# Attention in chunks of 64 tokens, with 64 x 64 products on quarters of TensorE's array

## The chip, the cores and the metric

The kernel runs on one core of a Trainium2 chip. The metric is device time in microseconds for one call. All inputs are float32; the big projections are computed in three passes on rounded halves, the attention products in plain f32.

## What is computed

Two layers over 2048 tokens of width 1024. Each projects the tokens, runs two groups of heads side by side, gates them, projects back and normalises. The change touches only the attention-like group of each layer: gated linear attention (GLA) in layer 0, retention in layer 1, both with 4 heads, key width 64 and value width 128. Cut to that part:

```python
def _gla(q, k, v, log_a):                       # layer 0, chunks of 64 tokens
    b = jnp.cumsum(log_a.reshape(B, n, C, H, dk), axis=2)
    q_dec, k_dec = q * jnp.exp(b), k * jnp.exp(-b)
    scores = jnp.where(causal, jnp.einsum('bnihd,bnjhd->bnhij', q_dec, k_dec), 0.0)
    o_intra = jnp.einsum('bnhij,bnjhe->bnihe', scores, v)
    k_state = k * jnp.exp(b_last[:, :, None] - b)
    chunk_state = jnp.einsum('bnjhd,bnjhe->bnhde', k_state, v)
    s_in = _chunk_scan(jnp.exp(b_last)[..., None], chunk_state)   # S <- decay * S + chunk_state
    return o_intra + jnp.einsum('bnihd,bnhde->bnihe', q_dec, s_in)

def _retention(q, k, v):                        # layer 1, the same form, a fixed decay per head
    scores = jnp.einsum('bnihd,bnjhd->bnhij', q, k) * dmat        # dmat: decay, causal
    o_intra = jnp.einsum('bnhij,bnjhe->bnihe', scores, v)
    chunk_state = jnp.einsum('bnjhd,hj,bnjhe->bnhde', k, w_state, v)
    return o_intra + jnp.einsum('bnihd,hi,bnhde->bnihe', q, w_inter, s_in)
```

The chunk length is free: a longer chunk does more inside the masked product, a shorter one more through the state.

## The kernel before

The tokens come in 4 blocks of 512 (`NB`), each of 4 tiles of 128 (`NT`). Per block the kernel runs layer 0 and then layer 1. A projection is a `unit`: 8 slices of the contraction (`kt`) times three passes, for two output tiles at a time, into PSUM tiles `big` (4 of them). Most of its matmuls are 512 wide; the first two units of layer 0 are 272 and 256 wide. Weights stream in as `raw` and are split by `cut` (ScalarE rounds, L89; VectorE subtracts, L90).

The order on every engine is that of the program text (the schedule is manual). Small work is put between projection matmuls: `later(fn, delay)` queues a step, and `between()`, called after each 24 wide matmuls of a two-tile unit, runs the steps that are due, in the order in which they were queued.

`attend` is used by both layers. It queues one `first` step and 4 `outputs` steps, one per tile. Heads are counted h = 2s + r: s says which 128-wide half of the keys holds the head, r whether its 64 key rows lie in partitions 0 to 63 or 64 to 127. `first` computes tile 0's scores (L357, `att<-G` or `att<-qkT`) and masks them into `pm`. `outputs(t)` does on TensorE:
- masked scores times values (`att<-v,pm`): 4 products with 128 rows and 128 columns;
- queries times state (`att<-s,G`, `att<-s,qkT`): 4 products with 64 rows;
- the next tile's scores (`att<-G`): 4 products with 64 rows, not in the last step;
- this tile's chunk states (L393, `trp<-v,G` or `trp<-v,ks`): 4 products with 64 columns.

Then come `norm` (statistics; in layer 0 squares on ScalarE, in layer 1 on VectorE, then GpSimd), the state update (an add, and the decay in `upd`), the mask for the next tile (L372), and `scale`, which reads the output out of PSUM. Scores and outputs of one step share two PSUM tiles `att`, one per r; each step takes both again. PSUM tiles `trp` (2 of them) serve the chunk states, transposes and small products.

The operands: in layer 0 `values` are copied from PSUM by ScalarE (L458, L487) and state keys are transposed by TensorE (L507) and copied (L508); in layer 1 values are copied at L700, and rotated keys by VectorE at L659.

Of the kernel before, what the change touches and what calls it, by code (L numbers as in the profile page):

```python
# [17 lines left out]
P = 128  # L18
# [33 lines left out]
def trunk(ctx, tc, x, xT, pos, wv, w, w_a2, pvec, rowp, sgu_rows, w_sT, w_pool, ropec, poolc, out):  # L52
    nc = tc.nc
# [12 lines left out]
    const = ctx.enter_context(tc.tile_pool(name="const", bufs=1))  # L66
# [77 lines left out]
    def later(fn, delay=1):  # L144
        steps.append([delay, fn])
# [63 lines left out]
    def layer_norm_out(xs, rows, lnrow, after, cuts=1):  # L209
# [6 lines left out]
        def evac(half, t, ps):  # L216
# [4 lines left out]
            if half == 1:  # L221
# [31 lines left out]
    pm = [const.tile([P, 4, P], F32, name=f"pm{i}") for i in range(2)]  # L253
# [18 lines left out]
    g128 = rope[:, 40:42]  # L272
# [11 lines left out]
    for kt in range(KT):  # L284
# [4 lines left out]
        t = wpool.tile([P, 2, 512], F32R, tag="w", name="wt")  # L289
# [61 lines left out]
            delay += 1  # L351


    def attend(qk, vt, state, upd, norm, delay):

        def mm(dst, lhsT, rhs, start=False, stop=False):
            nc.tensor.matmul(dst, lhsT=lhsT, rhs=rhs, start=start, stop=stop, skip_group_check=True)  # L357

        def banks():


            return [ps_s.tile([P, 4, P], F32, tag="s", name="att") for _ in range(2)]

        def scores(t, ps, start):
# [5 lines left out]
        def masked(t, ps):  # L370
            for r in range(2):
                nc.vector.copy_predicated(pm[t % 2][:, r::2, :], mask_b, ps[r][:, 2:4, :])  # L372

        def first():
            ps = banks()
            scores(0, ps, True)
            masked(0, ps)

        def outputs(t):
            v, m, ps = vt(t), pm[t % 2], banks()  # L380
            last = t == NT - 1
            for h in range(4):
                mm(ps[h % 2][:, h // 2, :], m[:, h, :], v[:, h * P:(h + 1) * P], start=h < 2)
            for s in range(2):
                for r in range(2):
                    b0 = 64 * r
                    mm(ps[r][:, s, :], qk(s, b0, t)[1], state[b0:b0 + 64, s, :], stop=last and s == 1)
            if not last:
                scores(t + 1, ps, False)
            u = tr()  # L390
            for h in range(4):
                s, b0 = h // 2, 64 * (h % 2)
                nc.tensor.matmul(u[b0:b0 + 64, s, :], lhsT=qk(s, b0, t)[2], rhs=v[:, h * P:(h + 1) * P],  # L393
                                 start=True, stop=True)
            scale = norm(t, [p_[:, 0:2, :] for p_ in ps])
            nc.vector.tensor_tensor(state, state, u[:, 0:2, :], op=ALU.add)
            upd(t)
            if not last:
                masked(t + 1, ps)
            scale()  # L400

        later(first, delay)
        for t in range(NT):
            later(lambda t=t: outputs(t), delay + 2 * t + 1)


    def gla_decay(alrT):
# [37 lines left out]
    def layer0(b, xs):  # L445

        vt = r8.tile([P, NT, 512], F32, tag="r8", name="v0")
        alrT = w2("alrT")[0:48, :].bitcast(F32R)
        als, logs, decays, heads = [], [], [], {}
        f = small.tile([P, 2, NT], F32, tag="f", name="f", bufs=2)  # L450

        def evac_v0(t, ps):
# [3 lines left out]
            nc.vector.tensor_copy(al[:, 32:48], al[:, 0:16])  # L456
            als.append(al)
            nc.scalar.activation(vt[:, t, 0:256], ps[:, 0:256], AF.Copy)  # L458

        def low_rank():  # L460
            pa = tr()
# [22 lines left out]
        later(low_rank, 1)  # L484
        later(decay, 2)
        later(decay2, 3)
        unit(xs, lambda t, ps: nc.scalar.activation(vt[:, t, 256:512], ps, AF.Copy), True, cols=256)  # L487


        held = {}  # L490
# [1 line left out]
        def evac_qk(n, ps):  # L492
            held[n] = ps
            if n % 2 == 0:
                return
            s = n // 2
            psq, psk = held[n - 1], ps

            G = r8.tile([P, 3, TB], F32, tag="r8", name=f"G{s}")
            e, ei, _ = decays[s]  # L500
            nc.vector.tensor_tensor(G[:, 1, :], psk, ei, op=ALU.mult)
            nc.vector.tensor_tensor(G[:, 0, :], psq, e, op=ALU.mult)

            def state_keys():
                pt = tr()
                for t in range(NT):
                    nc.tensor.transpose(pt[:, t, :], G[:, 1, t * P:(t + 1) * P], ident)  # L507
# [6 lines left out]

        def qk(s, b0, t):
            G, rows_, cols_ = heads[s], slice(b0, b0 + 64), slice(t * P, (t + 1) * P)
            return G[rows_, 1, cols_], G[rows_, 0, cols_], G[:, 2, t * P + b0:t * P + b0 + 64]

        def upd(t):
            nc.vector.tensor_tensor(s0, s0, f[:, :, t:t + 1].broadcast_to([P, 2, P]), op=ALU.mult)  # L520


        o1 = vt
# [86 lines left out]
        for i in range(2):  # L610
            r = r8.tile([P, 2, D], F32, tag="r8", name="rows")
# [23 lines left out]
    def layer1(b, xs, rows):  # L635

        qkT = z8.tile([P, NT, 4, P], F32, tag="z8", name="qkT")
        ks = [w2(f"ks{i}").rearrange("p (t c) -> p t c", c=256) for i in range(2)]
        kst = [ks[t // 2][:, t % 2, :] for t in range(NT)]
# [4 lines left out]
        def rotate(t, ps):  # L644
            g = b * NT + t
            a = w2("ra")
            s_ = w2("rs_")

            nc.scalar.activation(a[:, 0:256], ps[:, 0:256], AF.Copy)
            nc.vector.tensor_tensor(a[:, 256:512].rearrange("p (h c) -> p h c", c=64),  # L650
                                    ps[:, 256:512].rearrange("p (h c) -> p h c", c=64),
                                    gam[:, 4:8].unsqueeze(2).broadcast_to([P, 4, 64]), op=ALU.mult)
            a3 = a.rearrange("p (h c) -> p h c", c=32)
            s3 = s_.rearrange("p (h c) -> p h c", c=32)
            nc.vector.tensor_tensor(s3, a3, sin[:, g:g + 1, :].broadcast_to([P, 16, 32]), op=ALU.mult)
            nc.vector.tensor_tensor(a3, a3, cos[:, g:g + 1, :].broadcast_to([P, 16, 32]), op=ALU.mult)
            nc.vector.tensor_tensor(a3[:, 0::2, :], a3[:, 0::2, :], s3[:, 1::2, :], op=ALU.subtract)
            nc.vector.tensor_tensor(a3[:, 1::2, :], a3[:, 1::2, :], s3[:, 0::2, :], op=ALU.add)
            nc.vector.tensor_copy(kst[t], a[:, 256:512])  # L659

            def turn():
                pt = tr()
                for s in range(4):
                    nc.tensor.transpose(pt[:, s, :], a[:, s * P:(s + 1) * P], ident)  # L664
# [5 lines left out]

        def qk(s, b0, t):
            b1 = b0 + 64
            return qkT[b0:b1, t, 2 + s, :], qkT[b0:b1, t, s, :], kst[t][:, s * P + b0:s * P + b1]

        def upd(t):
            nc.vector.tensor_tensor(s1, s1, g128.unsqueeze(2).broadcast_to([P, 2, P]), op=ALU.mult)

# [176 lines left out]
```

## Time and profile before

| | |
|---|---|
| time, median of 3 runs | 1503.72 us (1502.76 to 1504.43) |
| the profiled execution | 1503.44 us, its span 1501.7 us |
| TensorE matmul, busy | 1482.5 us, 99% |
| VectorE, busy | 930.1 us, 62% |
| ScalarE, busy | 551.5 us, 37% |
| GpSimd, busy | 125.1 us, 8% |
| granted TensorE clock, mean | 0.996 |

In the rows of the profile, PE is TensorE's matmul, PEld its weight load, DVE is VectorE, ACT ScalarE, POOL GpSimd. A row of the timeline has the start and the length in us, the engine, the line, the operation, out<-in with the shape, and how many instructions were merged. "64*128" on a matmul is rows by columns of the stationary operand. An f32 product shows as two matmul records, a projection pass as one. A row of the groups has busy time, mean ns of one, and after the second bar the idle time of the engine just before them, with what ended it.

### The profile page before, as it was taken

How to read it: one execution, taken by the hardware profiler on the slowest of the kernel's cores; microseconds unless marked ns; L12 is line 12 of the kernel's file. 1: busy time of each engine (PE TensorE's matmuls, PEld its weight loads, DVE VectorE, ACT ScalarE, POOL GpSimd, SP SyncE). 2: the span in 40 equal slices, each digit the busy share in tenths (PEclk: the TensorE clock that was granted, in tenths of full speed). 3: DMA queues.
4: the chain of work that ended last, by engine and by line, in shares of the span. 5: the costliest groups of instructions: out<-in, count | busy, mean ns of one | idle time of the engine just before them, and what ended most of it. 6: DMA issues, size and time to landing. Idle time of an engine off the chain costs nothing.

```text
span 1501.7 us, 20886 instructions
## 1 busy us (share of the span) xinstructions
PE 1482.5 (99%) x7728; PEld 1246.0 (83%) x7728; DVE 930.1 (62%) x1856; ACT 551.5 (37%) x956; POOL 125.1 (8%) x184
## 2 busy tenths in 40 slices
PE   7999999999999999999999999999999999999997
PEld 6888888888988888888898888888889888888886
DVE  4586486656655458576665546857576554684755
ACT  5434323333543332334263342323426334142430
POOL 1020010000101001010111100000010110100002
PEclk9999999999999999999999999999999999999999
DMA  7324322225523341313453343132435315232321
GB/s 236 99 85 136 117 85 85 85 57 163 177 83 105 120 141 57 113 57 107 131 171 99 84 133 120 59 111 65 142 107 168 111 57 167 86 93 76 97 79 56
DMA packets 87046, 162.18 MB, mean 108 GB/s; under 512 B 10096, under 2 KB 18336, under 8 KB 86944
## 3 DMA queue, kind: packets, MB, share of 16 engines
q1 hardware_dynamic: 86944, 160.85, 34.6%
q8 instruction: 60, 0.98, 0.3%
q14 instruction: 42, 0.34, 0.1%
HBM read 152.43 MB, written 8.39 MB: 107 GB/s over the span
## 4 chain that ended last, share of the span: by engine, by line
PE 96%; DMA 2%; DVE 1%; issue 0%; POOL 0%; ACT 0%; SPq 0%; DVEq 0%; POOLq 0%; ACTq 0%
PE big L181 86%; PE att L357 4%; PE trp L393 1%; PE trp L574 1%; PE trp L626 1%; PE trp L716 1%; DMA xraw<-in_xT 1%; DMA raw<-in_w 1%; PE trp L664 0%; PE trp L752 0%; PE trp L601 0%; DVE wt L90 0%; DMA raw<-in_wv 0%; PE trp L507 0%; SPq L109 0%
## 5 line engine op out<-in xcount | busy, mean ns | idle before, releaser
L181 PE MATMUL big<-wt,T 128*128 128x512 f32 (+2 forms) x3456 | 726.2, 370 | 10.7 <-ACT v L458 5.9
L181 PEld LDWEIGHTS big<-wt,T 128*128 128x128 f32 x3456 | 599.5, 190 | 117.5 <-ACT v L458 6.2
L181 PE MATMUL big<-T,wt 128*128 128x512 f32 x2688 | 625.9, 392 | 0.0
L181 PEld LDWEIGHTS big<-T,wt 128*128 128x128 f32 x2688 | 500.9, 188 | 106.0 <-issue 2.7
L90 DVE TENSOR_TENSOR wt<-raw,wt 128x512 fp32r<-128x512 f32 (+1 forms) x496 | 320.7, 673 | 233.1 <-ACT wt L89 231.9
L89 ACT ACTIVATE wt<-raw 128x512 fp32r<-128x512 f32 (+1 forms) x496 | 297.8, 616 | 359.1 <-PE big L181 251.5
L198 POOL TENSOR_SCALAR lnrs<-lnmv 128x1 f32<-128x1 f32 x32 | 33.4, 1042 | 618.3 <-DVE lnmv L223 618.3
L219 DVE SCALAR_TENSOR_TENSOR rows<-rows,big 128x512 f32<-128x512 f32 x64 | 43.7, 682 | 55.6 <-PE big L181 55.6
L201 POOL TENSOR_TENSOR rs<-rs,neghalf 128x4 f32<-128x4 f32 x48 | 58.4, 1216 | 3.9
L628 ACT ACTIVATE T<-trp 128x512 fp32r<-128x512 f32 x32 | 17.4, 595 | 106.3 <-PE trp L626 106.3
L231 DVE SCALAR_TENSOR_TENSOR rows<-rows,lnrs,ln 128x1024 f32<-128x1024 f32 (+1 forms) x36 | 41.6, 1165 | 19.5 <-POOL lnrs L201 18.6
L220 DVE BATCH_NORM_STATS2 lnst<-rows 128x6 f32<-128x512 f32 x64 | 44.5, 695 | 2.2
L228 DVE SCALAR_TENSOR_TENSOR rows<-rows,lnmv,ln 128x1024 f32<-128x1024 f32 x32 | 41.0, 1283 | 0.9
L206 DVE SCALAR_TENSOR_TENSOR y<-trp,pv,sg 128x512 f32<-128x512 f32 x48 | 33.8, 745 | 12.4 <-PE trp L601 7.0
L372 DVE COPY_PREDICATED pm<-mask,att 128x256 f32<-128x256 int32 x64 | 24.6, 440 | 27.1 <-PE att L357 27.1
L724 ACT ACTIVATE pb<-big 128x512 f32<-128x512 f32 x16 | 9.4, 590 | 76.4 <-PE big L181 76.4
L586 ACT ACTIVATE act<-big 128x512 f32<-128x512 f32 x32 | 18.3, 597 | 51.7 <-PE big L181 50.9
L687 DVE BATCH_NORM_STATS2 st<-att 128x6 f32<-128x128 f32 x64 | 14.2, 286 | 35.4 <-PE att L357 35.4
L357 PEld LDWEIGHTS att<-v,pm 128*128 128x128 f32 x256 | 33.5, 191 | 2.4
L552 DVE BATCH_NORM_STATS2 st<-zt 128x6 f32<-128x128 f32 x64 | 13.7, 277 | 35.0 <-ACT zt L548 35.0
L729 DVE TENSOR_TENSOR pl<-pb 128x527 f32<-128x527 f32 x16 | 11.3, 708 | 38.6 <-ACT pb L724 37.8
L89 ACT ACTIVATE T<-y 128x512 fp32r<-128x512 f32 x48 | 29.4, 627 | 15.7 <-DVE y L206 15.3
(184 smaller groups left out, 903.7 us busy)
## 6 DMA issues: line engine op xcount, KB each, us to landing
raw<-in_w SPq DMA_DIRECT2D x448, 256.0 KB, 2.8
xraw<-in_xT SPq DMA_DIRECT2D x32, 256.0 KB, 3.5
rows<-in_x SPq DMA_DIRECT2D x8, 1024.0 KB, 7.5
ln<-in_rowp SPq DMA_DIRECT2D x16, 512.0 KB, 6.3
out<-rows SPq DMA_DIRECT2D x12, 512.0 KB, 2.7
raw<-in_wv SPq DMA_DIRECT2D x32, 136.0 KB, 3.3
raw<-in_wv SPq DMA_DIRECT2D x32, 128.0 KB, 3.0
out<-rows SPq DMA_DIRECT2D x8, 256.0 KB, 2.0
```

The costliest lines, as they stand in the source:

```text
L89: nc.scalar.activation(hi, src, AF.Copy)
L90: nc.vector.tensor_tensor(lo, src, hi.bitcast(F32), op=ALU.subtract)
L181: nc.tensor.matmul(p_, lhsT=lhsT, rhs=rhs, start=(kt == 0 and q == 0), stop=(kt == KT - 1 and q == 2))
L198: nc.gpsimd.tensor_scalar(dst, var, eps, None, op0=ALU.add)
L201: nc.gpsimd.tensor_tensor(dst, dst, neghalf[:, :n], op=ALU.pow)
L206: nc.vector.scalar_tensor_tensor(y, psT, gain, sil, op0=ALU.mult, op1=ALU.mult)
L219: nc.vector.scalar_tensor_tensor(rh, rh, ALPHA, ps, op0=ALU.mult, op1=ALU.add)
L220: nc.vector.bn_stats(sts[t][:, half, :], rh)
L228: nc.vector.scalar_tensor_tensor(row, row, mv[:, 0:1], gt, op0=ALU.subtract, op1=ALU.mult)
L231: nc.vector.scalar_tensor_tensor(row[:, cs], row[:, cs], rs, bt[:, cs], op0=ALU.mult, op1=ALU.add)
L357: nc.tensor.matmul(dst, lhsT=lhsT, rhs=rhs, start=start, stop=stop, skip_group_check=True)
L372: nc.vector.copy_predicated(pm[t % 2][:, r::2, :], mask_b, ps[r][:, 2:4, :])
```

## The change

A tile of 128 tokens becomes two chunks of 64, c = 0 and 1. Every attention product becomes two or more of 64 rows by 64 columns, addressed by (r, c): r picks the array's rows, c its columns. For the values and state keys this needs odd heads (r = 1) in partitions 64 to 127 and even heads in 0 to 63, for both chunks; so copies that were one instruction become four (`by_heads`). The exception is the scores, where r picks both the rows and the output partitions.

The state now has a middle value: `s_mid` after the first chunk, and two alternating ends, `state` and `s_odd`. Chunk states of tile t + 1 are computed in `outputs(t)`, those of tile 0 in `first`, and added in `prepare`, so the state stands a tile ahead. The last step has no chunk states. Chunk states take both `trp` tiles instead of one.

```diff
-    mask_b = mask.bitcast(I32).unsqueeze(1).broadcast_to([P, 2, P])
+    nc.gpsimd.tensor_copy(mask[64:128, 0:64], mask[64:128, 64:128])
+    mask_b = mask.bitcast(I32)[:, 0:64].unsqueeze(1).broadcast_to([P, 4, 64])
...
+    def by_heads(copy, dst, src):
+        for r in range(2):
+            for c in range(2):
+                copy(r, dst(r, c), src(c, r))
...
         def scores(t, ps, start):
-            for s in range(2):
-                for r in range(2):
-                    k, q = qk(s, 64 * r, t)[:2]
-                    mm(ps[r][:, 2 + s, :], k, q, start=start and s == 0, stop=s == 1)
+            for c in range(2):
+                for s in range(2):
+                    for r in range(2):
+                        k, q = qk(s, 64 * r, t)
+                        mm(ps[r][half(r), 2 + c, half(s)], k[:, half(c)], q[:, half(c)],
+                           start=start and c == 0 and s == 0, stop=True)
+        def chunk_states(t):
+            u = [tr(), tr()]
+            for s in range(2):
+                for c in range(2):
+                    for r in range(2):
+                        mm(u[r][half(c), s, :], kt(s, r, c, t), vals(t, s, r, c), start=s == 0, stop=True)
+            return u
+        def prepare(t, ps, u):
+            after = states[(t + 1) % 2]
+            for r in range(2):
+                nc.vector.copy_predicated(pm[t % 2][half(r)], mask_b[half(r)],
+                                          ps[r][half(r), 2:4, :].rearrange("p c (s i) -> p (c s) i", i=64))
+            for dst, src, c in ((s_mid, states[t % 2], 0), (after, s_mid, 1)):
+                for r in range(2):
+                    nc.vector.tensor_tensor(dst[half(r)], src[half(r)], u[r][half(c), 0:2, :], op=ALU.add)
+            upd(t, after)
...
         def outputs(t):
-            for h in range(4):
-                mm(ps[h % 2][:, h // 2, :], m[:, h, :], v[:, h * P:(h + 1) * P], start=h < 2)
             for s in range(2):
-                for r in range(2):
-                    mm(ps[r][:, s, :], qk(s, b0, t)[1], state[b0:b0 + 64, s, :], stop=last and s == 1)
+                for c in range(2):
+                    for r in range(2):
+                        mm(ps[r][half(c), s, :], m[half(r), 2 * c + s, :], vals(t, s, r, c), start=s == 0)
+            for s in range(2):
+                for c in range(2):
+                    for r in range(2):
+                        mm(ps[r][half(c), s, :], qk(s, 64 * r, t)[1][:, half(c)],
+                           (states[t % 2], s_mid)[c][half(r), s, :], stop=True)
             if not last:
                 scores(t + 1, ps, False)
-            u = tr()
-            for h in range(4):
-                nc.tensor.matmul(u[b0:b0 + 64, s, :], lhsT=qk(s, b0, t)[2], rhs=v[:, h * P:(h + 1) * P],
-                                 start=True, stop=True)
+                u = chunk_states(t + 1)
             scale = norm(t, [p_[:, 0:2, :] for p_ in ps])
-            nc.vector.tensor_tensor(state, state, u[:, 0:2, :], op=ALU.add)
-            upd(t)
             if not last:
-                masked(t + 1, ps)
+                prepare(t + 1, ps, u)
             scale()
...
-            nc.scalar.activation(vt[:, t, 0:256], ps[:, 0:256], AF.Copy)
+            values(t, ps, 0)
...
-                nc.scalar.activation(G[:, 2, :], flat(pt), AF.Copy)
+                kt4 = G[:, 2, :].rearrange("p (t c i) -> p t c i", c=2, i=64)
+                by_heads(act_copy, lambda r, c: kt4[half(r), :, c, :], lambda c, r: pt[half(c), :, half(r)])
...
-        attend(qk, lambda t: vt[:, t, :], s0, upd, norm, 2)
+        attend(qk, kt, lambda t: vt[:, t, :], s0, upd, norm, (2, 3, 5, 7, 9))
...
-            nc.vector.tensor_copy(kst[t], a[:, 256:512])
+            by_heads(dve_copy, lambda r, c: kd[half(r), c], lambda c, r: ka[half(c), :, r, :])
...
-        attend(qk, lambda t: vts[t], s1, upd, norm, 2)
-        unit(xs, lambda t, ps: nc.scalar.activation(vts[t], ps, AF.Copy), True)
+        attend(qk, kt, lambda t: vts[t], s1, upd, norm, (3, 4, 5, 7, 9))
+        unit(xs, values, True)
```

All matmuls of `attend` now have one line, L385. In layer 0's first block the values' first half is copied by ScalarE for r = 0 and by VectorE for r = 1 (`both_copy`).

On TensorE, `outputs(1)` of layer 0's first block stands before like this (out<-in, the output's partitions by elements, count of products; G are the two halves of queries and keys, s the state, v the values):

```order
L357 MATMUL att<-v_229,pm_111 128x128 x4
L357 MATMUL att<-s_114,G_651 128x128 x2
L357 MATMUL att<-s_114,G_750 128x128 x2
L357 MATMUL att<-G_651 128x128 x2
L357 MATMUL att<-G_750 128x128 x2
L393 MATMUL trp<-v_229,G_651 64x128 x2
L393 MATMUL trp<-v_229,G_750 64x128 x2
```

and now like this:

```order
L385 MATMUL att<-v_232,pm_112 64x128 x8
L385 MATMUL att<-s_odd,G_678 64x128 x2
L385 MATMUL att<-s_mid,G_678 64x128 x2
L385 MATMUL att<-s_odd,G_780 64x128 x2
L385 MATMUL att<-s_mid,G_780 64x128 x2
L385 MATMUL att<-G_678 64x64 x2
L385 MATMUL att<-G_780 64x64 x2
L385 MATMUL att<-G_678 64x64 x2
L385 MATMUL att<-G_780 64x64 x2
L385 MATMUL trp<-v_232,G_678 64x128 x4
L385 MATMUL trp<-v_232,G_780 64x128 x4
```

Sixteen products became 32, all 64 by 64 on the array, with no other shape between them.

On TensorE at the start of layer 1's attention, before (qkT holds queries and keys, ra a rotated tile that is transposed):

```order
L664 MATMUL trp<-ident,ra 128x128 x4
L357 MATMUL att<-qkT 128x128 x4
L181 MATMUL big<-wt,T 128x512 x24
L357 MATMUL att<-v_2224,pm_110 128x128 x4
L357 MATMUL att<-s_116,qkT 128x128 x4
L357 MATMUL att<-qkT 128x128 x4
L393 MATMUL trp<-v_2224,ks_2006 64x128 x4
L181 MATMUL big<-wt,T 128x512 x24
L181 MATMUL big<-T,wt 128x512 x24
L357 MATMUL att<-v_2224,pm_111 128x128 x4
```

and now:

```order
L718 MATMUL trp<-ident,ra 128x128 x4
L181 MATMUL big<-wt,T 128x512 x24
L385 MATMUL att<-qkT 64x64 x8
L385 MATMUL trp<-v_2349,ks_2119 64x128 x8
L181 MATMUL big<-wt,T 128x512 x24
L385 MATMUL att<-v_2349,pm_111 64x128 x8
L385 MATMUL att<-s_117,qkT 64x128 x2
L385 MATMUL att<-s_mid,qkT 64x128 x2
L385 MATMUL att<-s_117,qkT 64x128 x2
L385 MATMUL att<-s_mid,qkT 64x128 x2
L385 MATMUL att<-qkT 64x64 x8
L385 MATMUL trp<-v_2349,ks_2119 64x128 x8
```

The first step and `outputs(0)` each moved 24 wide matmuls later, while `outputs(1)` stayed: between `outputs(0)` and `outputs(1)` 24 wide matmuls stand now, 48 before.

On VectorE between those two steps of layer 1, before:

```order
L687 BN_STATS st<-att 128x6 x4
L689 BN_AGGR mv<-st 128x2 x4
L396 TENSOR_TENSOR s_116<-s_116,trp 128x256
L676 TENSOR_TENSOR s_116<-s_116,rope 128x256
L372 COPY_PREDICATED pm_111<-mask,att 128x2x128 x2
L695 TENSOR_SCALAR v_2224<-att,mv,rs 128x128 x4
```

and now:

```order
L744 BN_STATS st<-att 128x6 x4
L746 BN_AGGR mv<-st 128x2 x4
L413 COPY_PREDICATED pm_112<-mask,att 64x256 x2
L417 TENSOR_TENSOR s_mid<-s_odd,trp 64x256 x2
L417 TENSOR_TENSOR s_117<-s_mid,trp 64x256 x2
L733 TENSOR_TENSOR s_117<-s_117,rope 128x256
L752 TENSOR_SCALAR v_2349<-att,mv,rs 128x128 x4
```

The mask comes ahead of the state, one add became four on 64 partitions each, and `scale` follows them.

More of the change, by code (lines that the diff above doesn't have):

```diff
@@ L252, in trunk @@
     nc.gpsimd.memset(neghalf, -0.5)
-    pm = [const.tile([P, 4, P], F32, name=f"pm{i}") for i in range(2)]
+    pm = [const.tile([P, 4, 64], F32, name=f"pm{i}") for i in range(2)]
     for t in pm:
@@ L259, in trunk @@
     nc.gpsimd.memset(s1, 0.0)
+    s_odd = const.tile([P, 2, P], F32, name="s_odd")
+    s_mid = const.tile([P, 2, P], F32, name="s_mid")
     carry = const.tile([P, 4, 16], F32, name="carry")
@@ L351, in angles, with half, act_copy, dve_copy @@
             delay += 1
-    def attend(qk, vt, state, upd, norm, delay):
+    def half(n):
+        return slice(64 * n, 64 * n + 64)
+    def by_heads(copy, dst, src):
+        for r in range(2):
+            for c in range(2):
+                copy(r, dst(r, c), src(c, r))
+    def act_copy(r, dst, src):
+        nc.scalar.activation(dst, src, AF.Copy)
+    def dve_copy(r, dst, src):
+        nc.vector.tensor_copy(dst, src)
+    def both_copy(r, dst, src):
+        (act_copy, dve_copy)[r](r, dst, src)
+    def attend(qk, kt, vt, state, upd, norm, delays):
+        states = [state, s_odd]
         def mm(dst, lhsT, rhs, start=False, stop=False):
@@ L376, in first @@
             scores(0, ps, True)
-            masked(0, ps)
+            prepare(0, ps, chunk_states(0))
         def outputs(t):
-            v, m, ps = vt(t), pm[t % 2], banks()
+            m, ps = pm[t % 2], banks()
             last = t == NT - 1
-            for h in range(4):
-                mm(ps[h % 2][:, h // 2, :], m[:, h, :], v[:, h * P:(h + 1) * P], start=h < 2)
             for s in range(2):
-                for r in range(2):
-                    b0 = 64 * r
-                    mm(ps[r][:, s, :], qk(s, b0, t)[1], state[b0:b0 + 64, s, :], stop=last and s == 1)
+                for c in range(2):
[6 more added lines that the diff above has]
+                           (states[t % 2], s_mid)[c][half(r), s, :], stop=True)
             if not last:
                 scores(t + 1, ps, False)
-            u = tr()
-            for h in range(4):
-                s, b0 = h // 2, 64 * (h % 2)
-                nc.tensor.matmul(u[b0:b0 + 64, s, :], lhsT=qk(s, b0, t)[2], rhs=v[:, h * P:(h + 1) * P],
-                                 start=True, stop=True)
+                u = chunk_states(t + 1)
             scale = norm(t, [p_[:, 0:2, :] for p_ in ps])
-            nc.vector.tensor_tensor(state, state, u[:, 0:2, :], op=ALU.add)
-            upd(t)
             if not last:
-                masked(t + 1, ps)
+                prepare(t + 1, ps, u)
             scale()
-        later(first, delay)
+        later(first, delays[0])
         for t in range(NT):
-            later(lambda t=t: outputs(t), delay + 2 * t + 1)
+            later(lambda t=t: outputs(t), delays[t + 1])
     def gla_decay(alrT):
@@ L450, in layer0, with values @@
         f = small.tile([P, 2, NT], F32, tag="f", name="f", bufs=2)
+        def values(t, ps, s):
+            by_heads(both_copy if b == 0 and s == 0 else act_copy,
+                     lambda r, c: vt[half(r), t, (2 * c + s) * P:(2 * c + s + 1) * P],
+                     lambda c, r: ps[half(c), r * P:(r + 1) * P])
         def evac_v0(t, ps):
@@ L486, in layer0 @@
         later(decay2, 3)
-        unit(xs, lambda t, ps: nc.scalar.activation(vt[:, t, 256:512], ps, AF.Copy), True, cols=256)
+        unit(xs, lambda t, ps: values(t, ps, 1), True, cols=256)
         held = {}
@@ L516, in qk, with kt, upd @@
             G, rows_, cols_ = heads[s], slice(b0, b0 + 64), slice(t * P, (t + 1) * P)
-            return G[rows_, 1, cols_], G[rows_, 0, cols_], G[:, 2, t * P + b0:t * P + b0 + 64]
-        def upd(t):
-            nc.vector.tensor_tensor(s0, s0, f[:, :, t:t + 1].broadcast_to([P, 2, P]), op=ALU.mult)
+            return G[rows_, 1, cols_], G[rows_, 0, cols_]
+        def kt(s, r, c, t):
+            return heads[s][half(r), 2, t * P + 64 * c:t * P + 64 * c + 64]
+        def upd(t, st):
+            nc.vector.tensor_tensor(st, st, f[:, :, t:t + 1].broadcast_to([P, 2, P]), op=ALU.mult)
         o1 = vt
@@ L658, in rotate @@
             nc.vector.tensor_tensor(a3[:, 1::2, :], a3[:, 1::2, :], s3[:, 0::2, :], op=ALU.add)
-            nc.vector.tensor_copy(kst[t], a[:, 256:512])
+            ka = a[:, 256:512].rearrange("p (s r i) -> p s r i", r=2, i=64)
+            kd = kst[t].rearrange("p (c s i) -> p c s i", s=2, i=64)
+            by_heads(dve_copy, lambda r, c: kd[half(r), c], lambda c, r: ka[half(c), :, r, :])
             def turn():
@@ L672, in qk, with kt, upd @@
             b1 = b0 + 64
-            return qkT[b0:b1, t, 2 + s, :], qkT[b0:b1, t, s, :], kst[t][:, s * P + b0:s * P + b1]
-        def upd(t):
-            nc.vector.tensor_tensor(s1, s1, g128.unsqueeze(2).broadcast_to([P, 2, P]), op=ALU.mult)
+            return qkT[b0:b1, t, 2 + s, :], qkT[b0:b1, t, s, :]
+        def kt(s, r, c, t):
+            return kst[t][half(r), 128 * c + 64 * s:128 * c + 64 * s + 64]
+        def upd(t, st):
+            nc.vector.tensor_tensor(st, st, g128.unsqueeze(2).broadcast_to([P, 2, P]), op=ALU.mult)
         o1 = r8.tile([P, NT, 512], F32, tag="r8", name="v1")
@@ L697, in norm, with values @@
             return scale
-        attend(qk, lambda t: vts[t], s1, upd, norm, 2)
-        unit(xs, lambda t, ps: nc.scalar.activation(vts[t], ps, AF.Copy), True)
+        def values(t, ps):
+            pv4 = ps.rearrange("p (s r i) -> p s r i", r=2, i=P)
+            vd = vts[t].rearrange("p (c s i) -> p c s i", s=2, i=P)
+            by_heads(act_copy, lambda r, c: vd[half(r), c], lambda c, r: pv4[half(c), :, r, :])
+        attend(qk, kt, lambda t: vts[t], s1, upd, norm, (3, 4, 5, 7, 9))
+        unit(xs, values, True)
         cc, cd = act_unit(), act_unit()
```

4 lines of the change are left out of this document (2 added, 2 removed).

## The prediction

> **What bounds the kernel now.** I read the page's shares and the chain first, then the groups by form, then TensorE's timeline around attention.
>
> ```profile
> PE 1482.5 (99%) x7728; PEld 1246.0 (83%) x7728; DVE 930.1 (62%) x1856; ACT 551.5 (37%) x956; POOL 125.1 (8%) x184
> PE big L181 86%; PE att L357 4%; PE trp L393 1%; PE trp L574 1%; PE trp L626 1%; PE trp L716 1%; DMA xraw<-in_xT 1%; DMA raw<-in_w 1%; PE trp L664 0%; PE trp L752 0%; PE trp L601 0%; DVE wt L90 0%; DMA raw<-in_wv 0%; PE trp L507 0%; SPq L109 0%
> L181 PE MATMUL big<-T,wt 128*128 128x512 f32 x2688 | 625.9, 392 | 0.0
> L181 PE MATMUL big<-wt,T 128*128 128x512 f32 x2688 | 625.8, 392 | 0.0
> ```
>
> TensorE is busy all the time, the chain is TensorE's own work, and the 5376 wide projection matmuls never sat idle before a start. So TensorE's time in attention lies wholly on the path, as long as the other engines stay hidden. One attention of layer 0 (second block), a start of a wide stretch with no attention ahead of it, and a last step:
>
> ```profile
> 441.68 2.20 PE L181 MATMUL big<-wt,T 128*128 128x512 f32 x9
> 443.81 0.72 PE L357 MATMUL att<-G 64*128 64x128 f32 x8
> 444.46 5.74 PE L181 MATMUL big<-wt,T 128*128 128x512 f32 x24
> 450.04 1.05 PE L357 MATMUL att<-v,pm 128*128 128x128 f32 x8
> 451.02 0.71 PE L357 MATMUL att<-s,G 64*128 64x128 f32 x8
> 451.57 0.61 PE L357 MATMUL att<-G 64*128 64x128 f32 x8
> 452.11 0.66 PE L393 MATMUL trp<-v,G 128*64 128x128 f32 x8
> 452.70 1.65 PE L181 MATMUL big<-wt,T 128*128 128x512 f32 x6
> ...
> 458.27 5.60 PE L181 MATMUL big<-T,wt 128*128 128x512 f32 x24
> 463.71 1.05 PE L357 MATMUL att<-v,pm 128*128 128x128 f32 x8
> ...
> 492.86 1.05 PE L357 MATMUL att<-v,pm 128*128 128x128 f32 x8
> 493.84 0.71 PE L357 MATMUL att<-s,G 64*128 64x128 f32 x8
> 494.48 0.66 PE L393 MATMUL trp<-v,G 128*64 128x128 f32 x8
> 495.07 1.20 PE L181 MATMUL big<-T,wt 128*128 128x512 f32 x4
> ```
>
> Each f32 product is two records, so x8 is four products. What the rows give:
> - Wide matmuls: 463.71 - 458.27 = 5.44 us for 24, 0.227 each. Behind an attention step the 24 take 450.04 - 444.46 = 5.58, so 0.13 more.
> - Full products (128 rows, 128 columns): 1.05 = 7 gaps + one length of 0.27, so 0.11 us a record.
> - The 64-row products: 0.61 less 0.27 leaves 3 gaps of 0.11 for eight records: the two heads of a pair run side by side, two records every 0.11. The 64-column products (L393) go two by two as well.
> - A step's cost is its rows' starts plus that 0.13: a middle step 452.70 - 450.04 + 0.13 = 2.79 us, a last one 495.07 - 492.86 + 0.13 = 2.34.
>
> Changing the shape costs extra, seen when the timeline is cut finely:
>
> ```profile
> 443.50 0.39 PE L181 MATMUL big<-wt,T 128*128 128x512 f32 x1
> 443.81 0.38 PE L357 MATMUL att<-G 64*128 64x128 f32 x2
> ...
> 450.81 0.28 PE L357 MATMUL att<-v,pm 128*128 128x128 f32 x1
> 451.02 0.49 PE L357 MATMUL att<-s,G 64*128 64x128 f32 x4
> ```
>
> 443.81 - 443.50 is 0.31 where a wide matmul needs 0.227, and 451.02 - 450.81 is 0.21 where a full product needs 0.11: about 0.09 a change. On top, the first pair's weights are not hidden: s,G takes 0.71 (gaps 0.43, not 0.33: +0.10 with 128 columns), v,G 0.66 (+0.05 with 64). A first step thus costs 444.46 - 443.81 + 0.13 + 0.09 = 0.87. With 24 middle, 8 last and 8 first steps (4 blocks, 2 layers) attention costs 67.0 + 18.7 + 7.0 = 93 us.
>
> **TensorE's part of the change.** A middle step goes from 16 products to 32 of 64 x 64. The four (r, c) quarters take the masked scores times values, the queries times state and the chunk states: 8 products each over 4 quarters, two rounds of products, 4 rounds of records. Whether four quarters run at once no row shows; the nearest rows are the pairs by rows and the pairs by columns, both side by side at 0.11, and a quarter is one of each. The bounds are a round of 0.11 for four, or for two; I take four, since both halvings show no loss. The streams stay 128 wide, so a round stays 0.11. The scores are different: key rows and output partitions are both picked by r, so they lie on two quarters alone, 8 rounds of 2. Their stream is 64 wide. Bounds: half of 0.11 (0.055, if it scales) and 0.11 (if it doesn't). I take 0.06, because all load rows and streams above scale with columns.
>
> Middle step: entry 0.09, exposed weights 0.05, 12 rounds x 0.11 = 1.32, scores 8 x 0.06 = 0.48, exit 0.09 + 0.13; the same count for the step now gives 2.75 where 2.79 is measured, so 0.04 more: 2.20. Two shape changes inside the step go. Saved 0.59 x 24 = 14.2. Last step (8 rounds, no scores, its chunk states done earlier): 0.09 + 0.05 + 0.88 + 0.22 + 0.03 = 1.27, saved 1.07 x 8 = 8.6. First step (scores and chunk states): 0.09 + 0.05 + 0.44 + 0.48 + 0.22 + 0.02 = 1.30, lost 0.43 x 8 = 3.4. Sum: 19.4 saved. With scores at 0.11: 0.40 more in 32 steps, 12.8, leaving 6.6. At 0.055: 20.7.
>
> The Trainium skill, TensorEngine Tiling (Array Packing), Key Properties, says that tiles run independently and that another mode drains the array; by it the sum above stands at four at once. The 0.09 per change agrees, the four at once no run here shows.
>
> **VectorE.** Per step, four adds on 64 partitions replace one on 128 and the mask stays two instructions; 256 elements per partition each, so I price them at the full ones' rows. Layer 1 is where it is tight: its first step moves one slot later, and outputs(0) and outputs(1) then stand 24 wide matmuls apart, not 48.
>
> ```profile
> 269.02 1.05 PE L357 MATMUL att<-v,pm 128*128 128x128 f32 x8
> 270.55 0.61 PE L357 MATMUL att<-qkT 64*128 64x128 f32 x8
> ...
> 271.20 0.89 DVE L687 BATCH_NORM_STATS2 st<-att 128x6 f32<-128x128 f32 x4 [6.06 <-PE att L357]
> 272.00 0.36 DVE L689 BATCH_NORM_AGGREGATE mv<-st 128x2 f32<-128x6 f32 x4
> 272.28 0.39 DVE L396 TENSOR_TENSOR s<-s,trp 128x256 f32<-128x256 f32 x1
> 272.71 0.42 DVE L676 TENSOR_TENSOR s<-s,rope 128x256 f32<-128x256 f32 x1
> 273.05 0.77 DVE L372 COPY_PREDICATED pm<-mask,att 128x256 f32<-128x256 int32 x2
> 274.04 1.37 DVE L695 TENSOR_SCALAR v<-att,mv,rs 128x128 f32<-128x128 f32 x4 [0.22 <-POOL rs L201]
> ```
>
> VectorE starts when the scores end (270.55 + 0.61, then 271.20). From a step's start S, the new scores end at about S + 1.6. Statistics 1.08 (272.28 - 271.20), masks 0.7, adds 4 x 0.34 to 0.43 = 1.5, decay 0.4, scale 1.4: S + 6.7. The next step needs all of it, the scale too, because both banks are reused. It starts at S + 1.95 + 5.58 = S + 7.5. Slack 0.8 us, and VectorE has nothing else queued (its 6.06 idle). In layer 0 the first step is the near one:
>
> ```profile
> 445.97 0.75 DVE L372 COPY_PREDICATED pm<-mask,att 128x256 f32<-128x256 int32 x2
> 446.61 1.11 DVE L561 TENSOR_SCALAR zt<-zt,mv,rs 128x128 f32<-128x128 f32 x4
> ```
>
> Adds and decay follow the mask at 446.7 and end near 448.6, against outputs(0) at 450.04 plus the longer first step: 1.8 us to spare. Both chunk-state buffers of `trp` are held that long, and each next user (L574, L716) stands at least 24 wide matmuls off. So no wait: 0. In all VectorE gets 32 x 3 adds x 0.34 to 0.41, 33 to 39 us on 930, hidden. If the cover fails, 12 places wait: a microsecond late at each is 12 us.
>
> **ScalarE and the start.** Copies in quarters: values, state keys; VectorE's copies of keys likewise.
>
> ```profile
> 403.38 0.74 ACT L487 ACTIVATE v<-big 128x256 f32<-128x256 f32 x2 [0.46 <-PE big L181]
> 418.48 0.19 ACT L442 ACTIVATE ends<-ends 128x8 f32<-128x8 f32 x1
> 418.58 1.14 ACT L89 ACTIVATE wt<-raw 128x512 fp32r<-128x512 f32 x2
> 421.23 0.69 DVE L501 TENSOR_TENSOR G<-big,ta 128x512 f32<-128x512 f32 x1 [0.71 <-PE big L181]
> 24.48 1.59 ACT L458 ACTIVATE v<-big 128x256 f32<-128x256 f32 x4 [1.11 <-DVE alr L456]
> 24.91 2.50 PE L181 MATMUL big<-wt,T 128*128 128x256 f32 x10 [5.94 <-ACT v L458]
> ```
>
> A quarter copy lies between 0.10 (8 columns, 418.48 to 418.58) and 0.37 (256 columns); nearest is about 0.2, so 0.4 more per tile and 1.6 us ahead of the decay chain. That chain ends at 418.7, and L501 waits for TensorE until 421.2: hidden. At the start TensorE does wait for these copies; there two quarters go to VectorE. Bounds: 0 to two tiles x 0.37 = 0.7; I take 0.2.
>
> **Sum.** The profiled execution took 1503.4 us (span 1501.7), 0.3 below the median. 1503.4 - 19.4 + 0.2 = 1484.2.
>
> **Rivals.**
> - *Two at a time* (the other sign). TensorE runs no more than two small products at once, by shared operand paths or by instruction supply; the rows show no more than two per 0.11. Then 12, 8 and 4 rounds more per middle, last and first step: +1.32 x 24 + 0.88 x 8 + 0.44 x 8 = +42: 1526. If one matmul per 0.055 us is the floor, 64 per middle step take 3.5 us; with the one-quarter scores at 0.11 on top it is 12.8 more, 1539. It decides from 19.2 / 384 rounds = 0.05: a round of 0.16 wipes the gain out. For it: the doubled instruction count, 128 with loads in about 1.8 us, which nothing in this trace asks. Against: no gap opens in 24 records at 0.055. The Trainium skill, TensorE: Matmul & The Clock Gate, section "Wait — 56ns, not 53.3ns?", gives about 62 ns of sequencer work per matmul with hardware decode off; held to that, 64 matmuls would need 4.0 us and the kernel would end, by estimate, near 1553. The 0.055 above is under it, over a short stretch.
> - *Scores don't shrink* (0.11 a round): 1497. The one row for 64 columns (v,G) has the stream still 128 wide.
> - *VectorE late*: slack 0.8 misjudged by 1 to 2 us at 12 places: 1496 to 1508, about no change.
>
> **Chances.** A measurement here tells 0.2% (3 us) from no change. Forecast 0.58 (own range 1480 to 1490), scores 0.13, VectorE late 0.09, two at a time 0.20. Faster: 0.58 + 0.13 + half of VectorE's = 0.75; same 0.05; slower 0.20. The range takes all but the slow case and a little below: 1478 to 1510.
>
> **What would show it.** The new attention line's timeline: rows of eight with 128 columns in two gaps' time less than now (four records at one start), scores rows of 16 records near 0.7 us, middle steps of 2.2, last 1.3, first 1.3 with the same additions. Wide matmuls with idle 0.0 still; if they or attention wait on VectorE in layer 1's second step, the third rival is on. Middle steps over 3 us mean two at a time, and the forecast is wrong.

## The result and the profile after

The changed kernel takes 1510.55 us (median of 4, 1509.87 to 1512.27) against 1503.24: ratio 1.0051, 95% interval 1.0036 to 1.0066. It is slower; 1484 was forecast. Its profiled execution has a span of 1508.3 us, 6.6 more than before. The shares and the chain of the page, and the groups by form, are now these; behind them stand two lines of the kernel before, its chain by engine and its pooling product:

```profile
PE 1472.0 (98%) x8752; PEld 1226.2 (81%) x8752; DVE 985.4 (65%) x2008; ACT 594.9 (39%) x1116; POOL 116.3 (8%) x185
PE 84%; DVE 6%; ACT 4%; issue 2%; DMA 1%; POOL 1%; SPq 1%; DVEq 0%; POOLq 0%; ACTq 0%
L181 PE MATMUL big<-T,wt 128*128 128x512 f32 x2688 | 630.6, 393 | 5.6 <-ACT v L370 5.6
L181 PE MATMUL big<-wt,T 128*128 128x512 f32 x2688 | 625.6, 391 | 0.0
L778 PE MATMUL trp<-T,wp 128*128 128x512 f32 x48 | 15.8, 474 | 9.5 <-DVE s L417 9.5
...
PE 96%; DMA 2%; DVE 1%; issue 0%; POOL 0%; ACT 0%; SPq 0%; DVEq 0%; POOLq 0%; ACTq 0%
L716 PE MATMUL trp<-T,wp 128*128 128x512 f32 x48 | 12.5, 395 | 0.0
```

TensorE is busy 10.5 us less, and yet the span is longer. The chain, 96% TensorE's before, now goes through VectorE and ScalarE for a tenth of the span, and two groups have idle time ahead of them that had none: the wide matmuls wait 5.6 us for value copies, the pooling product (L778, L716 before) 9.5 us for the state adds.

TensorE's own part went as worked out. A middle step of layer 0, in the timeline:

```profile
453.24 0.67 PE L385 MATMUL att<-v,pm 64*64 64x128 f32 x16
453.73 0.28 PE L385 MATMUL att<-s,G 64*64 64x128 f32 x2
...
454.17 0.57 PE L385 MATMUL att<-G 64*64 64x64 f32 x13
454.52 0.33 PE L385 MATMUL trp<-v,G 64*64 64x128 f32 x2
...
454.63 0.62 PE L385 MATMUL trp<-v,G 64*64 64x128 f32 x14
455.18 5.05 PE L181 MATMUL big<-wt,T 128*128 128x512 f32 x21
```

Sixteen records of masked scores times values are through in 453.73 - 453.24 = 0.49 us, which is four rounds of 0.11 and 0.05 of exposed weights: four quarters run at once. The state products take 454.17 - 453.73 = 0.44. The step takes 455.18 - 453.24 = 1.94 from its first start to the next wide matmul, 2.66 before.

To find where the time went, I matched the 6144 projection matmuls of both traces one by one and took the differences of their starts. The steps of attention, with entry and exit, cost 2.149 us (middle, 2.78 before), 1.261 (last, 2.335) and 1.261 (first, 0.86): 24 x 0.633 + 8 x 1.074 - 8 x 0.401 = 20.6 us gained. The losses lie at four places:

| place | lost, us |
|---|---|
| pooling product of layer 1, 4 blocks (3.05, 4.00, 3.99, 3.99) | 15.0 |
| third output tile of the queries-and-keys unit in layer 0, blocks 1 to 3 | 7.4 |
| low-rank transposes and product, blocks 1 to 3 | 3.2 |
| the start, up to the first attention | 1.6 |

27.2 lost and 20.6 gained is the 6.6 of the span.

The largest, on TensorE and VectorE in layer 1 of the second block:

```profile
653.63 5.73 PE L181 MATMUL big<-T,wt 128*128 128x512 f32 x24
661.59 2.76 PE L778 MATMUL trp<-T,wp 128*128 128x512 f32 x6 [2.23 <-DVE s L417]
664.14 2.02 PE L181 MATMUL big<-T,wt 128*128 128x512 f32 x6
...
651.54 2.17 DVE L791 TENSOR_TENSOR pl<-pl 128x525 f32<-128x525 f32 x3
...
655.75 2.49 DVE L90 TENSOR_TENSOR wt<-raw,wt 128x512 fp32r<-128x512 f32 x4
658.16 0.88 DVE L744 BATCH_NORM_STATS2 st<-att 128x6 f32<-128x128 f32 x4
...
659.24 0.85 DVE L413 COPY_PREDICATED pm<-mask,att 64x256 f32<-64x256 int32 x2
660.12 0.86 DVE L417 TENSOR_TENSOR s_mid<-s_odd,trp 64x256 f32<-64x256 f32 x2
661.02 0.88 DVE L417 TENSOR_TENSOR s<-s_mid,trp 64x256 f32<-64x256 f32 x2
```

and the same place before:

```profile
654.32 0.66 PE L393 MATMUL trp<-v,ks 128*64 128x128 f32 x8
660.49 1.56 PE L716 MATMUL trp<-T,wp 128*128 128x512 f32 x6
...
658.80 0.89 DVE L687 BATCH_NORM_STATS2 st<-att 128x6 f32<-128x128 f32 x4
659.88 0.39 DVE L396 TENSOR_TENSOR s<-s,trp 128x256 f32<-128x256 f32 x1
```

The attention step was done on TensorE before 653.63, but VectorE comes to its statistics only at 658.16: the pooling windows (L791) and four weight cuts (L90) stand ahead in its queue. VectorE was as late before: its statistics started at 658.80, 4.5 us after TensorE had begun the chunk states at 654.32, but the chunk states held only one of the two `trp` tiles, up to the one add at 659.88, and the pooling product at 660.49 didn't wait. Now they hold both, and the adds stand behind the masks. The third of the four adds frees the first of them near 661.5, and L778, due at about 653.63 + 5.73 = 659.36, needs one. After the wait the clock falls. The windows (busy time of PE, PEld, DVE, ACT and POOL, then PEclk, the share of the DMA engines and GB/s):

```profile
655.80:661.50 5.70, 3.56 (x16) 2.63 (x14) 5.56 (x19) 4.98 (x9) 1.21 (x2) 1.00 0.58 184
661.60:664.10 2.50, 2.50 (x6) 1.99 (x7) 2.45 (x7) 0.87 (x2) 0.00 (x0) 0.53 0.00 1
664.10:665.10 1.00, 1.00 (x4) 0.77 (x3) 1.00 (x3) 0.00 (x0) 0.00 (x0) 0.50 0.00 0
```

Granted half speed for about 3.4 us, the product takes 2.76 us instead of 1.56 and the first wide matmuls behind it 0.43 instead of 0.23. This stretch is the part of the loss that is not waiting. The Trainium skill, TensorE: Matmul & The Clock Gate, section "What's actually happening", has the clock halved after an idle window of about 3.4 us. Here 2.23 us without a matmul was enough. The length of the wait alone doesn't decide it: in the first block the same product waited 2.83 us, and the granted clock behind it stayed at 1.00 (291.30:294.70), which is why that block lost 3.05 us and not 4.

The second place: ScalarE first, then TensorE in the changed kernel, and last ScalarE before.

```profile
421.99 2.25 ACT L370 ACTIVATE v<-big 64x128 f32<-64x128 f32 x8
423.15 0.96 PE L181 MATMUL big<-T,wt 128*128 128x512 f32 x3 [1.68 <-ACT v L370]
...
419.63 0.63 ACT L487 ACTIVATE v<-big 128x256 f32<-128x256 f32 x2
```

The second-half values of tiles 2 and 3 stand behind the decay chain on ScalarE. Before, they were out of PSUM at 419.63 + 0.63 = 420.26, and TensorE took those tiles again 48 wide matmuls of 0.227 after 410.12, at 421.0. Now eight quarters take 2.25 us, 0.28 each, and TensorE waits for both tiles. At the low-rank product it is the first-half copies:

```profile
399.79 2.25 ACT L370 ACTIVATE v<-big 64x128 f32<-64x128 f32 x8 [1.43 <-DVE alr L504]
...
403.24 0.59 ACT L512 ACTIVATE alrT<-trp 48x512 fp32r<-48x512 f32 x1
...
403.88 0.73 PE L455 MATMUL trp<-alrT,wa 48*128 48x512 f32 x2 [0.53 <-ACT alrT L512]
```

### The profile page after: what moved, and what is told of

The parts are those of the page before. It is cut to its first block, busy times and chain, and to the rows that moved or that the text cites. A ratio compares the mean times of both kernels' runs of the same rounds, so it can differ in the third digit from the quotient of the medians.

```text
span 1508.3 us, 23315 instructions
## 1 busy us (share of the span) xinstructions
PE 1472.0 (98%) x8752; PEld 1226.2 (81%) x8752; DVE 985.4 (65%) x2008; ACT 594.9 (39%) x1116; POOL 116.3 (8%) x185
## 4 chain that ended last, share of the span: by engine, by line
PE 84%; DVE 6%; ACT 4%; issue 2%; DMA 1%; POOL 1%; SPq 1%; DVEq 0%; POOLq 0%; ACTq 0%
PE big L181 76%; PE att L385 3%; DVE wt L90 2%; ACT v L370 1%; DVE pl L791 1%; PE trp L778 1%; PE trp L626 1%; PE trp L678 1%; ACT wt L89 1%; PE trp L385 1%; DMA raw<-in_wv 1%; DVE ta L472 0%; SPq L109 0%; PE trp L718 0%; PE trp L814 0%
## 5 line engine op out<-in xcount | busy, mean ns | idle before, releaser
L90 DVE TENSOR_TENSOR wt<-raw,wt 128x512 fp32r<-128x512 f32 (+1 forms) x496 | 318.0, 672 | 247.3 <-ACT wt L89 246.0
L370 ACT ACTIVATE v<-big 64x128 f32<-64x128 f32 (+1 forms) x184 | 56.6, 308 | 35.0 <-PE big L181 17.7
L201 POOL TENSOR_TENSOR rs<-rs,neghalf 128x4 f32<-128x4 f32 x48 | 49.3, 1028 | 3.9
L791 DVE TENSOR_TENSOR pl<-pb 128x527 f32<-128x527 f32 x16 | 11.3, 708 | 32.6 <-ACT pb L786 31.8
L90 DVE TENSOR_TENSOR T<-y,T 128x512 fp32r<-128x512 f32 x48 | 31.6, 688 | 0.5
```

What stands on the lines that cost most here:

```text
L90: nc.vector.tensor_tensor(lo, src, hi.bitcast(F32), op=ALU.subtract)
L201: nc.gpsimd.tensor_tensor(dst, dst, neghalf[:, :n], op=ALU.pow)
L370: nc.scalar.activation(dst, src, AF.Copy)
```

## The experiments

Theory A: these four waits are separate, each has its own cause, and each can be removed by itself. Theory B: VectorE and ScalarE have about 100 us more to do, and a wait taken away comes back where they are next needed.

**The pooling product one slot later** (behind the last attention step, where no chunk states hold the buffers):

```diff
-                    later(out, 1)
+                    later(out, 2 if half == 1 else 1)     # in pool_unit
```

> Theory A (waits): TensorE's attention is about 20.6 us shorter in the changed kernel, and 27 us are lost in waits of TensorE at four places. The largest is the pooling product of layer 1 (L778): it needs a trp buffer while both are held until the late state adds, 3.0 to 4.0 us a block, 15 us in all. Set one slot later, behind the last attention step, it should find the buffers free: 1495.5 us, 1493 to 1498, and no idle time ahead of L778. Theory B (load): VectorE and ScalarE have about 100 us more to do between them, and a wait taken away at one place comes back at the next one that shares them (the transposes L814, the last step): 1505 us or more.

1496.58 us, ratio 0.9957 (0.9940 to 0.9973). The wait is gone:

```profile
L778 PE MATMUL trp<-T,wp 128*128 128x512 f32 x48 | 12.9, 403 | 0.0
```

14.0 us less than the changed kernel, and this edit alone makes it faster than before. By the matched starts nothing is lost at this place any more. A holds here.

**The decay chain's second half one slot later**, so that the value copies go ahead of it on ScalarE:

```diff
-        later(decay2, 3)
+        later(decay2, 4)
```

> Theory A: the second place is the third pair of the queries-and-keys unit in layer 0, whose PSUM tiles are still held by value copies that stand behind the decay chain on ScalarE: 2.45 us in each of blocks 1 to 3, 7.4 us. With the chain's second half queued one slot later, the copies go ahead of it, in time in which ScalarE waited 2.1 us for VectorE: 1503 us, 1501 to 1505. Theory B: the chain ends later, the keys are scaled later, and TensorE waits at the transposes of the keys instead: 1508 us or more.

1500.83 us, ratio 0.9983 (0.9974 to 0.9992): 9.7 us less than the changed kernel, more than the 7.4 expected. The second place loses nothing any more, and the wide group's idle time is 0.0 again. The rest comes from elsewhere:

```profile
L181 PE MATMUL big<-T,wt 128*128 128x512 f32 x2688 | 627.1, 392 | 0.0
L778 PE MATMUL trp<-T,wp 128*128 128x512 f32 x48 | 14.0, 432 | 9.5 <-DVE s L417 9.5
```

The pooling product waits 9.5 us as it did, but by the matched starts it loses 3.04, 2.45, 3.97 and 2.47 us in the four blocks, 11.9 in all and not 15.0: the clock fell at one of these waits in this execution, at three in the changed kernel's. The same wait of 2.23 us costs 2.5 us or 4.0, as the clock stays up or falls. So 7.4 of the 9.7 us are the edit's aim, and the rest isn't its doing as far as the trace shows.

**First-half values over ScalarE and VectorE in all blocks:**

```diff
-            by_heads(both_copy if b == 0 and s == 0 else act_copy,
+            by_heads(both_copy if s == 0 else act_copy,
```

> In all blocks ScalarE copies only the even heads' first-half values in layer 0, VectorE the odd ones. Theory A: the low-rank transposes and the product behind them wait about 1.1 us less in each of blocks 1 to 3 (3.2 us), and the decay chain starts 1 us earlier, which takes 1 us a block off the second place: 1504 to 1508 us. Theory B: VectorE's copies cost what ScalarE's saved: 1509 to 1512.

1512.34 us, ratio 1.0056 (1.0041 to 1.0071): a miss for A, 1.8 above the changed kernel, just above B's range. TensorE, ScalarE and VectorE around the low-rank transposes:

```profile
401.32 0.29 PE L511 MATMUL trp<-ident,alr 128*48 128x128 f32 x1 [1.40 <-DVE alr L504]
...
399.59 0.56 ACT L370 ACTIVATE v<-big 64x128 f32<-64x128 f32 x2 [1.49 <-DVE alr L504]
...
400.18 0.59 DVE L373 COPY v<-big 64x128 f32<-64x128 f32 x2 [0.60 <-ACT v L370]
```

In this program the two engines read one PSUM tile only in turn: ScalarE waits for VectorE's `alr`, VectorE's copy for ScalarE's, and the next tile's `alr`, which the transposes need, stands behind that copy. The low-rank loss grows from 3.2 to 5.6 us, while the second place gives back 1.8. It isn't VectorE's load, it is the order.

**All three:**

> All three together. Theory A: 1510.5 - 15 - 7.4 - 3.2 = 1485 us, 1483 to 1490, which is what the forecast's TensorE terms alone gave. Theory B: 1497 or more, with new waits on VectorE or ScalarE.

1490.42 us, ratio 0.9912 (0.9897 to 0.9927), just outside A's range and far from B's: the third edit's 2.4 us are in it, and a slower start, in which the granted clock was half for 10.2 us (0.50 in 22.80:33.00), not for 6.8 as in the changed kernel's execution (0.51 in 23.40:30.30).

**The first two without the third:**

> The pooling product one slot later and the decay chain one slot later, with the values copied as in the changed kernel. The split of the first-half copies over both engines made things worse (ScalarE and VectorE take turns on one PSUM tile), by 1.65 to 1.97 us a block at the low-rank transposes where the changed kernel loses 0.86 to 1.16. Theory A: 1510.5 - 14 - 9.7 = 1486.8 us, 1485 to 1489, under the 1490.4 of all three. Theory B (a wait removed comes back elsewhere): 1490 or more.

1487.20 us, ratio 0.9892 (0.9877 to 0.9906), as A expected, in part by luck: the 9.7 in A's sum hold some 2 us that the clock at the pooling product gave, and the first edit has taken that loss away already; in their place the start was 1.7 us shorter in this execution. ScalarE in the second block:

```profile
410.18 2.26 ACT L370 ACTIVATE v<-big 64x128 f32<-64x128 f32 x8
412.45 1.28 ACT L482 ACT_TABLE_LOAD   x1
413.80 0.63 ACT L482 ACTIVATE tb<-ta 128x512 f32<-128x512 f32 x1
```

The copies fill the time in which ScalarE waited 2.06 us for VectorE ahead of L482; the chain isn't later for it.

**And the first-half copies of tiles 2 and 3 behind the low-rank step:**

```diff
             als.append(al)
-            values(t, ps, 0)
+            if b > 0 and t >= 2:
+                late.append((t, ps))
+            else:
+                values(t, ps, 0)
...
         later(low_rank, 1)
+        later(late_values, 1)      # values(t, ps, 0) for each in late
```

> As the last, and in blocks 1 to 3 the first-half value copies of tiles 2 and 3 go behind the low-rank step on ScalarE. Theory A: the low-rank product no longer waits for ScalarE; about 1 us less in each of 3 blocks: 1484 us, 1482 to 1486. Theory B: the copies push the decay chain back and the wait returns at the keys or the PSUM tiles: 1487 or more.

1485.56 us, ratio 0.9881 (0.9866 to 0.9896), the best version: 1.2% faster than the kernel before. In the second block ScalarE now has

```profile
396.86 0.59 ACT L521 ACTIVATE alrT<-trp 48x512 fp32r<-48x512 f32 x1 [1.10 <-PE trp L520]
397.35 2.26 ACT L370 ACTIVATE v<-big 64x128 f32<-64x128 f32 x8
```

and it is ScalarE that waits for the transposes. The low-rank loss is halved, 3.2 to 1.6; the rest is a wait of the transposes for `alr` that stays.

**The copies alone**, in the kernel before: values, state keys and rotated keys in quarters, to the places they had.

```diff
-            nc.scalar.activation(vt[:, t, 0:256], ps[:, 0:256], AF.Copy)
+            quarters(act_copy, vt[:, t, 0:256], ps[:, 0:256])   # 64 partitions x half the columns, four times
```

> The kernel before, with only the copies of values, state keys and rotated keys cut into quarters of 64 partitions by half the columns (same places, attention as before). Theory A: the losses at the queries-and-keys unit (2.45 us a block in 3 blocks), at the low-rank step (1.1 us a block in 3 blocks) and at the start (about 1 us) come from the copies alone: 1503.5 + 11 = 1514 us, 1511 to 1517, and nothing lost at the pooling product. Rival: they need the new attention's load too: 1503 to 1506.

1509.42 us, ratio 1.0039 (1.0024 to 1.0053): slower with the attention untouched, but 6 us where 11 were expected, between A's range and the rival's. Nothing is lost at the pooling product; the second place loses 4.5 us, the low-rank step 0.7, the start 0.9. In these rows

```profile
422.34 1.77 ACT L361 ACTIVATE v<-big 64x128 f32<-64x128 f32 x8
423.26 3.01 PE L181 MATMUL big<-T,wt 128*128 128x512 f32 x11 [0.97 <-ACT v L361]
```

the wait is the same kind, but eight quarters take 1.77 us, 0.22 each, and not 2.25.

**The copies alone, across partitions**, as the changed kernel lays them out:

```diff
-                copy(dst[64*r:64*r+64, c*w:c*w+w], src[64*r:64*r+64, c*w:c*w+w])     # in quarters
+                copy(dst[64*r:64*r+64, c*w:c*w+w], src[64*c:64*c+64, r*w:r*w+w])
```

> The kernel before with the copies in quarters as in the changed kernel's layout: half of them move data between the lower and the upper 64 partitions; the attention is left as it was and reads the moved data, so it computes other values. With quarters in place the copies took 0.22 us each and cost 6 us; in the changed kernel they took 0.28. Theory A: crossing partitions is what makes them 0.28, and the loss at the queries-and-keys unit grows from 1.1 to about 2.4 us a block: 1513 us, 1511 to 1516. Rival: 0.28 comes from the new attention's traffic: 1509 as before, with copies of 0.22.

1518.85 us, ratio 1.0101 (1.0084 to 1.0118), more than expected. The profiled execution took 1516.94: the low-rank step lost 3.6 us in it, and the start 2.3. The other three took about 2 us more, and what they lost it on no trace shows.

```profile
425.25 2.25 ACT L361 ACTIVATE v<-big 64x128 f32<-64x128 f32 x8
```

0.28 each again, with the old attention, so the layout of the copies does it and not the new attention. The first two copies of the row, in place in the last run and then across:

```profile
422.34 0.42 ACT L361 ACTIVATE v<-big 64x128 f32<-64x128 f32 x2
...
425.25 0.54 ACT L361 ACTIVATE v<-big 64x128 f32<-64x128 f32 x2
```

A single copy is as long in both, 0.26 us for the first. In place the second one starts before the first has ended, across it doesn't. In place the first two stay in one half of the partitions; across, the half that is read changes with every copy. Whether the crossing costs the overlap or this change of half, no run separates: the same crossing copies in an order that reads one half twice in a row weren't tried. The second place loses 7.5 us and the low-rank step 3.6, the changed kernel's 7.4 and 3.2. So these two losses come from the copies alone, and the layout's price is more than the number of instructions.

**The state adds ahead of the statistics**, in the changed kernel:

```diff
                 u = chunk_states(t + 1)
+                add_states(t + 1, u)       # the four adds, taken out of prepare
```

> The changed kernel with the four state adds ahead of the norm's statistics on VectorE (mask and decay stay behind), so that the two trp buffers come free earlier. Theory A, the pooling product waits for the buffers and nothing else: the adds now end about 1.2 us earlier (statistics 1.08 and masks 0.7 behind them, less about 0.5 for waiting on the chunk states), so that much less a block and less of the slow-clock stretch after it: 1503 to 1506 us. Rival, the wait is for VectorE's backlog in general (the windows of the pooling ahead of it): 1509 to 1511.

1503.15 us, ratio 0.9995 (0.9985 to 1.0004): 7.4 less than the changed kernel, at the good edge of A. VectorE and TensorE in the second block:

```profile
660.34 0.88 DVE L423 TENSOR_TENSOR s<-s_mid,trp 64x256 f32<-64x256 f32 x2
...
660.91 1.63 PE L784 MATMUL trp<-T,wp 128*128 128x512 f32 x6 [0.52 <-DVE s L423]
```

VectorE's work is the same and its backlog too; only the buffers come free sooner, and the wait falls from 2.23 to 0.52 us. The clock stayed up at all four of these waits, and the place loses 3.5 us in four blocks instead of 15.0. But in the third block it fell at the second place, behind a wait of only 1.69 us:

```profile
792.77 0.97 PE L181 MATMUL big<-T,wt 128*128 128x512 f32 x3 [1.69 <-ACT v L370]
...
794.40:797.80 3.40, 3.40 (x10) 2.61 (x9) 0.69 (x1) 0.66 (x2) 0.00 (x0) 0.50 0.18 46
```

That block lost 4.0 us there, the other two 2.5. (The scale, now later, makes layer 1's second step wait 0.45 us a block.)

**The order of the quarters:** s innermost, so that two products in a row share a quarter.

```diff
-            for s in range(2):
-                for c in range(2):
-                    for r in range(2):
+            for c in range(2):
+                for r in range(2):
+                    for s in range(2):
```

> The changed kernel with s as the innermost loop in the three groups that use all quarters, so that two products in a row go to the same quarter; the same products, loads and copies. What it tells: whether four at a time depends on the order in the program. If TensorE starts matmuls in the program's order, a group of 8 products takes about 1.1 us instead of 0.44 (five product times of 0.22, since only neighbours in different quarters overlap): +0.66 a group, 3, 2 and 1 groups in 24 middle, 8 last and 8 first steps: about 64 us, 1574. If it picks products out of order by quarter: no change, 1510.

One run, 1512.87 us. The step of the second block:

```profile
455.49 0.69 PE L385 MATMUL att<-v,pm 64*64 64x128 f32 x16
...
456.00 0.33 PE L385 MATMUL att<-s_mid,G 64*64 64x128 f32 x2
...
456.30 0.33 PE L385 MATMUL att<-s,G 64*64 64x128 f32 x2
...
457.49 0.74 PE L181 MATMUL big<-wt,T 128*128 128x512 f32 x2
```

2.00 us against 1.94. With starts in program order it would have been near 3.9. The rows show it directly: in this program all products with `s` stand ahead of those with `s_mid`, yet a record of `s_mid` starts at 456.00 and one of `s` as late as 456.30. So the order of the program text is not the order of starts on TensorE where products go to different quarters; those of other quarters are taken ahead, and the source order is worth only 0.06 us of this step.

## Why the prediction was wrong

- *TensorE's sum* was right: middle steps 2.149 (2.20 forecast), last 1.261 (1.27), first 1.261 (1.30); 20.6 us gained, 19.4 forecast. Four quarters at a time held, the scores' rounds came out near 0.06 (the second value I chose between bounds), and the shape change costs what it did. The forecast of 1484 is met within 2 us by the version with most of the waits taken away, 1485.56.
- *The rival of the other sign* had the wrong mechanism. Two at a time is excluded by the rows; the kernel got slower by another way, which no rival had.
- *The step that failed first*: "Both chunk-state buffers of `trp` are held that long, and each next user (L574, L716) stands at least 24 wide matmuls off. So no wait: 0." The time from a step to the adds was taken where VectorE idled 6.06 us ahead of it, layer 1's second step, and used for all. At the third step VectorE is 4.5 us behind, which the trace before showed in the same place. That cost 15.0 us, forecast at 0.
- *The step that failed second*: value copies "hidden". A quarter was priced at 0.2 us, between 0.10 and 0.37; it is 0.28. The cover named was the keys' scaling (L501), which waits for TensorE until 421.2. But the copies also hold PSUM tiles that TensorE takes again 0.74 us after the copies of before were through. That consumer was not looked for. With the low-rank step it cost 10.6 us, forecast at 0.
- *The third rival* (VectorE late) put the lateness in layer 1's second step, at 1 to 2 us. That step never waited: the slack of 0.8 us held. It was the right engine at the wrong consumer, one that a held buffer made wait.
- *The start* at 0.2 us: 1.6 in this execution, -0.1 to 3.3 in the others with the changed attention, whose start varies by more than that term, so what the copies cost there stays open. The three longest starts, 2.7 to 3.3, are those in which the clock was half for 10.2 us.
- *VectorE's sum* was too small, 55.3 us more busy time where 33 to 39 were forecast; this changed nothing, as the waits came from where VectorE stood and not from its total.

The experiments carry this: one moved step each takes away the first and second loss (14.0 us of the median for the first; 7.4 us by the matched starts for the second), the copies alone bring the second and third back in the old kernel, and all of it came without less work on VectorE or ScalarE.

## What to carry to other kernels

When a change makes a step hold one more buffer, list everyone who takes from that pool next, and for each the time at which the releasing engine gets there in its own queue at that place; the slack of one instance says nothing of the others. For an engine's longer copy, look at what it frees, not only at who reads what it writes. An engine at 65% can still be 4.5 us behind where it counts; there, moving one small step by a slot was worth 14.0 us, two thirds of what the change had saved on TensorE.

## What the runs showed of the hardware

A ScalarE copy of 64 x 128 out of PSUM takes 0.26 to 0.27 us. In a row of eight it came to 0.22 each where two in a row stayed in one half of the partitions, and to 0.28 where half of them crossed over and the half that was read changed with each. A copy of 128 x 256, four times the elements, took 0.26 back to back (two in 0.63 with the length of one at 0.37). Cutting a copy in quarters is thus close to four times the time.

Products on different quarters of the array start out of program order (456.00 for one of `s_mid`, 456.30 for one of `s` that stands ahead of it).

A TensorE wait of 2.23 us, in one block even one of 1.69 us, was followed by half the granted clock for about 3.4 us in some blocks and executions and not in others, so the price of one and the same wait of 2.23 us varied between 2.5 and 4.0 us. A wait of 2.83 us in the first block wasn't followed by it in any of the three executions that had it.
